# Seven block products in place of eight in the first four K tiles of fourteen block pairs

## The chip, the cores and the metric

The kernel runs on one core of a Trainium2 chip. The metric is the device time of one execution, in microseconds (us). The engines are named as the profile names them: PE (TensorE, matmuls), PEld (its weight loads), DVE (VectorE), ACT (ScalarE), POOL (GpSimd) and SP (the engine whose queue issues most DMAs).

## The reference

Two layers on a sequence of 256 tokens with 2048 features, in float32. Each is followed by a LayerNorm of the residual. The first is a gated MLP with a causal spatial gate, the second is stick-breaking attention with 16 heads.

```python
# layer 1: A_WIDTH 4096, 8 groups of 512 columns, chunks of 128 tokens
h = x @ w_in + b_in                      # w_in: 2048 x 12288
u, v, g = jnp.split(h, 3, axis=-1)
u = jax.nn.gelu(u)
v = layer_norm(jax.nn.gelu(v), vln_g, vln_b)
mixed = jnp.einsum('gts,bcsge->bctge', w, v) + b_s.T[None, None, :, :, None]
y = (u * mixed * jax.nn.silu(g)) @ w_out # 4096 x 2048
x = layer_norm(DN_ALPHA * x + y, ...)
# layer 2
k, v = jnp.split(x @ kv_w, 2, axis=-1)
q, g = jnp.split(x @ w_in, 2, axis=-1)
o = stick_breaking_attention(q, k, v)
x = layer_norm(DN_ALPHA * x + (o * jax.nn.silu(g)) @ w_out, ...)   # w_out: 2048 x 2048
```

## The kernel before

**Products.** A float32 product is made of three matmuls on operands that are split in a high and a low part (`mm3`, L86 to L90: high by high, high by low, low by high). The high part is a cast on ACT (`split`, L77), the low part is a subtraction on DVE (L78). The two token tiles of 128 are the stationary operand, and a matmul streams 512 weight columns. So a block of 512 output columns has two PSUM banks, one for each token tile, and per K tile of 128 rows six matmuls.

**Weights.** `load_chunk` (L115 to L139) loads two K tiles by 512 columns (512 KB) through SP's queue into a tile of the pool `wraw` (4 buffers), and splits it in two tiles of the pool `wspl` (`WB` = 5 buffers of each). `gemm` takes the chunks one after the other.

**Order.** The kernel is written as a program in the Tile framework. A scheduler puts each engine's instructions into an order of its own, by a simulated timeline, and adds the semaphores; the order of an engine's instructions is fixed when the kernel is built. Tiles of one pool and tag take turns in the pool's buffers. Nearly everything of the gated MLP that isn't a weight chunk shares one tag of 26 buffers of 4 KB per partition (pool `big`: the raw x tiles, v, vh and vl, u, g, zh and zl, wsh, wsl and wsr, the residual r, the LayerNorm rows lgb). PSUM has two pools of four banks: `ps_acc` for the products, `ps_aux` for transposes, mixing and attention.

**Stages.** First eight products of 512 columns give v (bias on DVE, Gelu on ACT, statistics on DVE). The spatial weights wsr are loaded and masked, v's LayerNorm factors are worked out. Then for each of 8 groups: v is normalised (L218, L219) and split into vh and vl; two products give u and g; the group's mixing matmuls take vh and vl; u is multiplied by the mix, g by u (`gate`, L305); eight PE transposes of g (L336) and a split give zh and zl, the stationary operand of the output projection. Which of u and g comes first alternates from group to group. After the groups come the output projection of the gated MLP (`residual_gemm`, 4 blocks of 512 columns, 32 K tiles), the first LayerNorm with transposes (xtp, L410), under which the first chunks of the attention's V product run, four rounds of attention (V, K, Q and gate products, and the stick-breaking work of four heads each), the attention's output projection (4 blocks, 16 K tiles) and the last LayerNorm.

Of the kernel before, what the change touches and what calls it, by code (L numbers as in the profile page):

```python
# [9 lines left out]
F32 = mybir.dt.float32  # L10
# [25 lines left out]
ACT_M = (1, 3)  # L36
PINS = {4: (0, 1), 5: (2, 3)}
WARM = 5


@with_exitstack
def trunk_kernel(ctx, tc, x, xT, w_in, b_in, vln_g, vln_b, w_sT, b_sT, w_out, kv_w, bw_in, bw_out, ln_g, ln_b, ln_gT, ln_bT, out):
    nc = tc.nc

    lead = ctx.enter_context(tc.tile_pool(name="lead", bufs=1))
    wraw = ctx.enter_context(tc.tile_pool(name="wraw", bufs=4))
    wspl = ctx.enter_context(tc.tile_pool(name="wspl", bufs=WB))
    big = ctx.enter_context(tc.tile_pool(name="big", bufs=26))
    bcp = ctx.enter_context(tc.tile_pool(name="bcp", bufs=3))
    const = ctx.enter_context(tc.tile_pool(name="const", bufs=1))  # L50
    small = ctx.enter_context(tc.tile_pool(name="small", bufs=4))
    ps_acc = ctx.enter_context(tc.tile_pool(name="ps_acc", bufs=4, space=PSUM))
    ps_aux = ctx.enter_context(tc.tile_pool(name="ps_aux", bufs=4, space=PSUM))

    uid = [0]

# [5 lines left out]
        return big.tile(shape, dt, tag="big", name=nm(s))  # L62

    def aux(s):
        return ps_aux.tile([P, NT], F32, tag="aux", name=nm(s))

    last_w = []

# [65 lines left out]

    def gemm(w, col0, nk, stat, evac, tail=0, head=0, ahead=None, halves=False, cuts=1, after=None):
        w_ = NT // cuts
        accs = [ps_acc.tile([P, w_ if tok else NT], F32, tag="acc", name=nm("acc")) for tok in range(NTOK)]
        wv = w.rearrange("(k p) n -> p k n", p=P)
        nch = nk // CK  # L139
        wh, wl = [None] * nch, [None] * nch  # L140

        def load(c):
            halve = halves and c == 0
            if ahead and not halve:
                ahead(c)
            wh[c], wl[c] = load_chunk(wv, c, col0, spill=nch - tail <= c < nch - WB or c < head - WB, ahead=ahead if halve else None)

        full = [(slice(0, NT), accs[0])], [(slice(0, w_), accs[1])]
        for i in range(1, cuts):
            full[1].append((slice(i * w_, (i + 1) * w_), ps_aux.tile([P, w_], F32, tag="aux", name=nm("acc"))))  # L150
# [24 lines left out]
        for c in range(head):  # L175
            use(c, [1])
        for c in range(head, nch - tail):
            load(c)
            use(c, both)
        for c in range(nch - tail, nch):  # L180
            load(c)
            use(c, [0])
        if tail:
            pins = evac(0, accs[0]) or {}
            for cs, acc in full[1]:
                for c in range(nch - tail, nch):
                    first = use(c, [1], (None, [(cs, acc)]))
                    for t in pins.get(c - (nch - tail), ()):
                        order(t, first)
                evac(1, acc, cs)  # L190
        else:
            for tok in both:
                evac(tok, accs[tok])

    def rsqrt_var(mv, s, fill=None):
        ve = small.tile([P, 1], F32, tag="ve", name=nm("ve"))
# [90 lines left out]
    for n in range(G):  # L287
# [7 lines left out]
            split(vh[:, tok, :], vl[:, tok, :], v[:, tok, :])  # L295

        u = big_tile([P, NTOK, NT], F32, "u")
        ubias = bcast(b_in[n * NT : (n + 1) * NT])

        gt = big_tile([P, NTOK, NT], F32, "g")  # L300
        gbias = bcast(b_in[2 * AW + n * NT : 2 * AW + (n + 1) * NT])
        u_last = n % 2 == 1

        def gate(tok, gt=gt, u=u):
            nc.vector.tensor_tensor(out=gt[:, tok, :], in0=gt[:, tok, :], in1=u[:, tok, :], op=ALU.mult)  # L305

        def evac_u(tok, acc, u=u, bias=ubias, vh=vh, vl=vl, n=n, last=u_last):
            nc.vector.tensor_tensor(out=u[:, tok, :], in0=acc, in1=bias, op=ALU.add)
            nc.scalar.activation(u[:, tok, :], u[:, tok, :], AF.Gelu_apprx_tanh)
            mp = aux("mix")  # L310
            mm3(mp, wsh[:, n, :], wsl[:, n, :], vh[:, tok, :], vl[:, tok, :], True, True)
            nc.vector.scalar_tensor_tensor(out=u[:, tok, :], in0=mp, scalar=bs[:, n : n + 1], in1=u[:, tok, :],
                                           op0=ALU.add, op1=ALU.mult)
            if last:
                gate(tok)

        def evac_g(tok, acc, gt=gt, bias=gbias, last=not u_last):
            nc.vector.tensor_tensor(out=gt[:, tok, :], in0=acc, in1=bias, op=ALU.add)
            nc.scalar.activation(gt[:, tok, :], gt[:, tok, :], AF.Silu)
            if last:  # L320
                gate(tok)

        parts = [(n * NT, evac_u), (2 * AW + n * NT, evac_g)]
        for col0, evac in parts[::-1] if u_last else parts:
            gemm(w_in, col0, KD, xstat, evac)

        zh = big_tile([P, HPT, S], F32R, "zh")
        zl = big_tile([P, HPT, S], F32R, "zl")
# [10 lines left out]
            split(zh[:, hs, :], zl[:, hs, :], tp.rearrange("p (k t) -> p k t", k=2))  # L339


    def residual_gemm(w, nk, stat, rt, layer, finish, fill=None, cuts=1):
        groups = 3 + cuts
        stats = [small.tile([P, groups, 6], F32, tag=f"st{tok}{cuts}", name=nm("st"), bufs=1) for tok in range(NTOK)]
        gb = []

        for n in range(4):
            last = n == 3

            def evac(tok, acc, cs=slice(0, NT), n=n, last=last):  # L350
                r = rt[n][:, tok, cs]
                with tc.high_priority():
                    nc.vector.scalar_tensor_tensor(out=r, in0=r, scalar=ALPHA, in1=acc, op0=ALU.mult, op1=ALU.add)
# [9 lines left out]
            if last:  # L363
                for m in range(4):
                    cs = slice(m * NT, (m + 1) * NT)
                    lt = big_tile([P, 2, NT], F32, "lgb")
                    g, b = lt[:, 0, :], lt[:, 1, :]
                    nc.gpsimd.dma_start(g, ln_g[layer, cs].partition_broadcast(P))
                    nc.gpsimd.dma_start(b, ln_b[layer, cs].partition_broadcast(P))
                    gb.append((g, b))  # L370
            gemm(w, n * NT, nk, stat, evac, tail=TAIL if last else 0, cuts=cuts if last else 1)
        return gb

    xv = x.rearrange("(c p) n -> p c n", p=P)
# [47 lines left out]
    def zstat(k):  # L422
        return zTh[k // HPT][:, k % HPT, :], zTl[k // HPT][:, k % HPT, :]

    gb0 = residual_gemm(w_out, KA, zstat, rt, 0, finish1, fill=fill1)


    nc.vector.memset(tri_f, -1.0)
# [23 lines left out]
                                    compare_op=ALU.is_ge, fill=0.0)  # L452

    sps, wts = [], []
    kw = dict(skip_group_check=True)

    def gemm_T(w, col0, evac, hook=None):
        accs = [ps_acc.tile([P, NT], F32, tag="acc", name=nm("acc")) for _ in range(2)]
# [67 lines left out]
    for j in range(4):  # L526
# [32 lines left out]
        z2s.append((z2h, z2l))  # L559
        for i in range(HPT // 2):  # L560
            weighted(i, v, sg, z2h, z2l)

    def z2stat(k):
        h, l = z2s[k // HPT]
# [18 lines left out]
                steps.append(center(tok, mv, gb, m + 3))  # L583
        order(*steps)

    residual_gemm(bw_out, KD, z2stat, rt, 1, finish2, fill=fill2, cuts=2)
# [38 lines left out]
```

## Time and profile before

| | |
|---|---|
| time, median of 3 runs | 1222.52 us (1222.43 to 1222.58) |
| time of the profiled execution | 1222.06 us |
| its span | 1220.4 us |
| v products | to 182 us |
| u and g products, 8 groups | 182 to 555 us |
| output projection of the gated MLP | 555 to 712 us |
| first LayerNorm | 712 to 750 us |
| attention | 750 to 1121.5 us |
| output projection of the attention | 1121.5 to 1209 us |
| last LayerNorm's end | 1209 to 1220.4 us |

The span runs from the first to the last instruction that the profiler saw; the time of the same execution holds 1.7 us more. Starts are counted from the span's start. Under a name such as `acc<-wh,xTh` stands what is written and what it is made from; in rows of PE the weights (wh, wl) and the tokens (xTh, xTl) are the operands of one matmul. A matmul's shown length (0.39 us) is modelled and overlaps the next one; the distance of starts says how fast matmuls follow each other.

### The profile page before, as it was taken

How to read it: one execution, taken by the hardware profiler on the slowest of the kernel's cores; microseconds unless marked ns; L12 is line 12 of the kernel's file. 1: busy time of each engine (PE TensorE's matmuls, PEld its weight loads, DVE VectorE, ACT ScalarE, POOL GpSimd, SP SyncE). 2: the span in 40 equal slices, each digit the busy share in tenths (PEclk: the TensorE clock that was granted, in tenths of full speed). 3: DMA queues.
4: the chain of work that ended last, by engine and by line, in shares of the span. 5: the costliest groups of instructions: out<-in, count | busy, mean ns of one | idle time of the engine just before them, and what ended most of it. 6: DMA issues, size and time to landing. Idle time of an engine off the chain costs nothing.

```text
span 1220.4 us, 16640 instructions
## 1 busy us (share of the span) xinstructions
PE 1206.5 (99%) x6597; PEld 1053.1 (86%) x6597; DVE 714.7 (59%) x789; ACT 582.7 (48%) x663; POOL 51.5 (4%) x94
## 2 busy tenths in 40 slices
PE   9999999999999999999999999999999999999996
PEld 6888888888888888888888889998998999999885
DVE  6655558667657657655554577455455555546566
ACT  6444445544544544544333455474464455456340
POOL 0000001000000000000000000010010000002000
PEclk9999999999999999999999999999999999999998
DMA  9776777676676677767655655645555655657651
GB/s 307 241 216 202 207 220 238 189 235 205 181 235 206 181 233 222 220 212 247 195 191 195 211 169 174 188 151 173 180 159 167 186 161 156 190 173 203 203 198 69
DMA packets 123694, 240.70 MB, mean 197 GB/s; under 512 B 8129, under 2 KB 11745, under 8 KB 123617
## 3 DMA queue, kind: packets, MB, share of 16 engines
q1 hardware_dynamic: 118848, 224.69, 58.4%
q0 software_dynamic: 4480, 14.70, 4.6%
q8 instruction: 51, 0.84, 0.3%
q10 hardware_dynamic: 288, 0.26, 0.1%
q14 instruction: 27, 0.21, 0.0%
HBM read 237.52 MB, written 2.10 MB: 196 GB/s over the span
## 4 chain that ended last, share of the span: by engine, by line
PE 98%; DVE 1%; DMA 1%; SPq 0%; DVEq 0%; issue 0%
PE acc L89 31%; PE acc L88 31%; PE acc L87 31%; PE ztp L336 1%; DMA xTr<-in_xT 1%; PE zp L501 0%; PE op L88 0%; PE zp L89 0%; PE op L87 0%; PE zp L88 0%; PE op L89 0%; PE zp L87 0%; PE zp L504 0%; PE mix L87 0%; PE mix L89 0%; PE mix L88 0%
## 5 line engine op out<-in xcount | busy, mean ns | idle before, releaser
L78 DVE TENSOR_TENSOR wl<-raw,wh 128x1024 fp32r<-128x1024 f32 (+1 forms) x417 | 507.6, 1223 | 444.0 <-ACT wh L77 442.8
L77 ACT CAST wh<-raw 128x1024 fp32r<-128x1024 f32 (+1 forms) x417 | 437.3, 1051 | 559.3 <-PE acc L89 371.8
L88 PE MATMUL acc<-wl,xTh 128*128 128x512 f32 x896 | 349.7, 391 | 0.0
L87 PE MATMUL acc<-wh,xTh 128*128 128x512 f32 x896 | 348.8, 391 | 0.9 <-ACT xTh L77 0.9
L89 PE MATMUL acc<-wh,xTl 128*128 128x512 f32 x896 | 348.9, 390 | 0.1
L88 PE MATMUL acc<-xTl,wh 128*128 128x256 f32 x768 | 217.4, 283 | 0.0
L87 PE MATMUL acc<-xTh,wh 128*128 128x256 f32 x768 | 217.3, 283 | 0.0
L89 PE MATMUL acc<-xTh,wl 128*128 128x256 f32 x768 | 217.2, 283 | 0.0
L87 PEld LDWEIGHTS acc<-wh,xTh 128*128 128x128 f32 x896 | 168.4, 188 | 36.8 <-ACT xTh L77 2.3
L89 PEld LDWEIGHTS acc<-wh,xTl 128*128 128x128 f32 x896 | 168.5, 188 | 35.2 <-DVE xTl L78 0.5
L88 PEld LDWEIGHTS acc<-wl,xTh 128*128 128x128 f32 x896 | 168.5, 188 | 34.4
L87 PEld LDWEIGHTS acc<-xTh,wh 128*128 128x128 f32 x768 | 147.2, 192 | 0.2
L88 PEld LDWEIGHTS acc<-xTl,wh 128*128 128x128 f32 x768 | 147.2, 192 | 0.2
L89 PEld LDWEIGHTS acc<-xTh,wl 128*128 128x128 f32 x768 | 147.1, 192 | 0.0
L87 PE MATMUL acc<-wh,zh 128*128 128x512 f32 x256 | 99.9, 390 | 0.0
L88 PE MATMUL acc<-wl,zh 128*128 128x512 f32 x256 | 99.7, 390 | 0.0
L89 PE MATMUL acc<-wh,zl 128*128 128x512 f32 x256 | 99.6, 389 | 0.0
L88 PEld LDWEIGHTS acc<-wl,zh 128*128 128x128 f32 x256 | 48.1, 188 | 9.9
L87 PEld LDWEIGHTS acc<-wh,zh 128*128 128x128 f32 x256 | 48.1, 188 | 9.9
L89 PEld LDWEIGHTS acc<-wh,zl 128*128 128x128 f32 x256 | 48.1, 188 | 9.8
L88 PE MATMUL acc<-wl,z2h 128*128 128x512 f32 (+1 forms) x144 | 52.7, 366 | 0.0
L87 PE MATMUL acc<-wh,z2h 128*128 128x512 f32 (+1 forms) x144 | 52.7, 366 | 0.0
(134 smaller groups left out, 745.5 us busy)
## 6 DMA issues: line engine op xcount, KB each, us to landing
raw<-in_w_in SPq DMA_DIRECT2D x191, 512.0 KB, 4.5
raw<-in_w_out SPq DMA_DIRECT2D x64, 512.0 KB, 4.5
raw<-in_kv_w SPq DMA_DIRECT2D x64, 512.0 KB, 3.7
raw<-in_bw_in SPq DMA_DIRECT2D x64, 512.0 KB, 3.8
raw<-in_bw_out SPq DMA_DIRECT2D x32, 512.0 KB, 4.4
bc<-in_b_in POOLq DMA_DIRECT2D x16, 256.0 KB, 4.7
bc<-in_b_in SPq DMA_DIRECT2D x8, 256.0 KB, 4.5
bc<-in_vln_g POOLq DMA_DIRECT2D x8, 256.0 KB, 4.9
```

Source lines behind the costliest of these rows:

```text
L77: h = nc.scalar.copy(hi, src)
L78: return h, nc.vector.tensor_tensor(out=lo, in0=src, in1=hi.bitcast(F32), op=ALU.subtract)
L87: first = nc.tensor.matmul(acc, lhsT=ah, rhs=bh, start=start, stop=False, **kw)
L88: nc.tensor.matmul(acc, lhsT=ah, rhs=bl, start=False, stop=False, **kw)
L89: nc.tensor.matmul(acc, lhsT=al, rhs=bh, start=False, stop=stop, **kw)
L336: nc.tensor.transpose(out=tp[:, (kk * NTOK + tok) * P : (kk * NTOK + tok + 1) * P], in_=gt[:, tok, c : c + P], identity=ident)
```

## The change

In fourteen pairs of 512-column blocks the first four K tiles no longer go through eight products of (token tile, K half, column block) but through seven, by a scheme of the Strassen and Winograd kind. The pairs are: v blocks 2 to 7 (three pairs), u and g of each group (eight), the output projection of the gated MLP (two), and blocks 0 and 1 of the attention's output projection (one). v blocks 0 and 1, blocks 2 and 3 of the last projection and the attention's products stay as they were.

Write a11, a12 for token tile 0 and K tiles 0-1 and 2-3, a21, a22 for token tile 1; x, y for the two column halves of the weights in K tiles 0-1, w, z for those in K tiles 2-3. The products are: P1 = a11·x, Q5 = (a21-a22)·(x+y), P2 = a12·w, P6 = (a21-a22-a11)·(x+y+z), P7 = (a11-a21)·(y+z), Q3 = (a12+a21-a22-a11)·z, Q4 = a22·(x+y+z+w). Each is six matmuls. Four of them (P1, Q5, P6, P7) leave partial sums in a bank that are copied out, by a DVE operation, into the output tile while the bank goes on accumulating (`snap`). The order of the products and of the remaining chunks of the two blocks is that of `plan`.

The sums on the token side are made once for the input, once for z and once for the attention's output (`a_forms`: one DVE addition of 128x1024, four DVE operations of 128x256 and a split). The sums on the weight side are DVE additions in place (128x1024) in the raw tiles. x is loaded into a tile of `big`, y, z and w into tiles of `wraw`. The bias rows of a pair go into a tile of `big`. `wraw` has 5 buffers where it had 4, `big` 25 where it had 26, and the two PSUM pools become one pool of eight banks with one tag. In the groups g is now always the block of half 0, which ends last, and u that of half 1. The LayerNorm rows of the last projections are loaded ahead of the tail.

```diff
+NP = 2
+
+
+def plan(nk, tail=0):
+
+    each = (nk - 2 * NP) // CK
+    one = ["P1", "Q5", "P2", 1, "P6", 1, "P7", 1, 1, "Q3"] + [1] * (each - 4)
+    zero = [0, "Q4"] + [0] * (each - tail - 1)
+    return one + zero
...
-    wraw = ctx.enter_context(tc.tile_pool(name="wraw", bufs=4))
+    wraw = ctx.enter_context(tc.tile_pool(name="wraw", bufs=5))
     wspl = ctx.enter_context(tc.tile_pool(name="wspl", bufs=WB))
-    big = ctx.enter_context(tc.tile_pool(name="big", bufs=26))
+    big = ctx.enter_context(tc.tile_pool(name="big", bufs=25))
...
-    ps_acc = ctx.enter_context(tc.tile_pool(name="ps_acc", bufs=4, space=PSUM))
-    ps_aux = ctx.enter_context(tc.tile_pool(name="ps_aux", bufs=4, space=PSUM))
+    ps = ctx.enter_context(tc.tile_pool(name="ps", bufs=8, space=PSUM))
...
+    def a_forms(h, l, p):
+
+        raw = big_tile([P, 2 * p, S], F32, "ar")
+        nc.vector.tensor_tensor(out=raw, in0=h.bitcast(F32), in1=l.bitcast(F32), op=ALU.add)
+        a11, a21, a12, a22 = [raw[:, k * p : (k + 1) * p, t * P : (t + 1) * P] for k in range(2) for t in range(2)]
+        f = big_tile([P, 4, p, P], F32, "af")
+        fh, fl = big_tile([P, 4, p, P], F32R, "afh"), big_tile([P, 4, p, P], F32R, "afl")
+        for i, (a, b, op) in enumerate([(a21, a22, ALU.subtract), (f[:, 0], a11, ALU.subtract),
+                                        (a11, a21, ALU.subtract), (a12, f[:, 1], ALU.add)]):
+            nc.vector.tensor_tensor(out=f[:, i], in0=a, in1=b, op=op)
+        split(fh, fl, f)
+        return fh, fl
+
+    def block(w, cols, nk, stat, forms, p, plan, snap, final, tail=0, before_tail=None):
+
+
+        wv = w.rearrange("(k p) n -> p k n", p=P)
+        b = [None] * 4
+
+        def load(k, half, keep=False):
+            r = big_tile([P, CK, NT], F32, "sraw") if keep else wraw.tile([P, CK, NT], F32, tag="raw", name=nm("raw"))
+            nc.sync.dma_start(r[:, 0:p, :], wv[:, k : k + p, cols[half] : cols[half] + NT])
+            return r[:, 0:p, :]
...
+        def product(i, src, a):
+            wh = wspl.tile([P, CK, NT], F32R, tag="wh", name=nm("wh"))
+            wl = wspl.tile([P, CK, NT], F32R, tag="wl", name=nm("wl"))
+            split(wh[:, 0:p, :], wl[:, 0:p, :], src)
+            acc, new = bank(i)
+            for j in range(p):
+                ah, al = a(j)
+                mm3(acc, ah, al, wh[:, j, :], wl[:, j, :], new and j == 0, j == p - 1, **kw)
+            return acc
...
+        def P1():
+            raw["x"], raw["y"], raw["z"] = load(0, 0, keep=True), load(0, 1), load(p, 1)
+            snap("P1", product(1, raw["x"], quarter(0, 0)))
+            add(raw["x"], raw["y"])
+
+        def Q5():
+            snap("Q5", product(2, raw["x"], form(0)))
+            add(raw["x"], raw["z"])
+            add(raw["y"], raw["z"])
+
+        def P2():
+            raw["w"] = load(p, 0)
+            product(0, raw["w"], quarter(p, 0))
+
+        def P6():
+            snap("P6", product(1, raw["x"], form(1)))
+            add(raw["x"], raw["w"])
+
+        def P7():
+            snap("P7", product(1, raw["y"], form(2)))
+
+        def Q3():
+            product(2, raw["z"], form(3))
+
+        def Q4():
+            product(1, raw["x"], quarter(p, 1))
...
+        for s in plan:
+            if isinstance(s, str):
+                steps[s]()
+                continue
+            k = left[s].pop(0)
+            wh, wl = load_chunk(wv, k // CK, cols[s])
+            use(s, k, wh, wl, (1, 0) if s else (0, 1))
+            if not left[s]:
+                for tok in range(NTOK):
+                    final(tok, s, b[2 * s + tok])
+        if tail:
+            before_tail()
...
+    def bias_block(w, cols, nk, stat, forms, p, plan, bias, dst, then):
+
+        def snap(name, acc):
+            tok, half = dict(P1=(0, 0), Q5=(1, 1), P6=(0, 1), P7=(1, 1))[name]
+            d = dst(tok, half)
+            if name == "P7":
+                nc.vector.tensor_tensor(out=d, in0=d, in1=acc, op=ALU.subtract)
+            elif name == "P6":
+                nc.vector.tensor_tensor(out=d, in0=bias[half], in1=acc, op=ALU.subtract)
+            else:
+                nc.vector.tensor_tensor(out=d, in0=acc, in1=bias[half], op=ALU.add)
+
+        def final(tok, half, acc):
+            d = dst(tok, half)
+            nc.vector.tensor_tensor(out=d, in0=acc, in1=bias[half] if (tok, half) == (1, 0) else d, op=ALU.add)
+            then(tok, half)
+
+        block(w, cols, nk, stat, forms, p, plan, snap, final)
...
+    def pair_bias(*cols):
+        t = big_tile([P, 2, NT], F32, "pb")
+        for i, c in enumerate(cols):
+            nc.gpsimd.dma_start(t[:, i, :], b_in[c : c + NT].partition_broadcast(P))
+        return [t[:, i, :] for i in range(2)]
...
-    for n in range(G):
+    for n in range(2):
...
+    xforms = a_forms(xTh[:, 0 : 2 * NP, :], xTl[:, 0 : 2 * NP, :], NP)
+    for n in range(2, G, 2):
+        pair = [big_tile([P, NTOK, NT], F32, "v") for _ in range(2)]
+        vt += pair
+        bias = pair_bias(AW + (n + 1) * NT, AW + n * NT)
+
+        def v_then(tok, half, pair=pair, n=n):
+            d = pair[1 - half][:, tok, :]
+            nc.scalar.activation(d, d, AF.Gelu_apprx_tanh)
+            nc.vector.bn_stats(vstats[:, tok, n + 1 - half, :], d)
+
+        bias_block(w_in, (AW + (n + 1) * NT, AW + n * NT), KD, xstat, xforms, NP, plan(KD), bias,
+                   lambda tok, half, pair=pair: pair[1 - half][:, tok, :], v_then)
...
+        cols = (2 * AW + n * NT, n * NT)
+
+        def ug_then(tok, half, gt=gt, u=u, vh=vh, vl=vl, n=n):
+            if half:
+                nc.scalar.activation(u[:, tok, :], u[:, tok, :], AF.Gelu_apprx_tanh)
+                mp = aux("mix")
+                mm3(mp, wsh[:, n, :], wsl[:, n, :], vh[:, tok, :], vl[:, tok, :], True, True)
+                nc.vector.scalar_tensor_tensor(out=u[:, tok, :], in0=mp, scalar=bs[:, n : n + 1], in1=u[:, tok, :],
+                                               op0=ALU.add, op1=ALU.mult)
+            else:
+                nc.scalar.activation(gt[:, tok, :], gt[:, tok, :], AF.Silu)
+                nc.vector.tensor_tensor(out=gt[:, tok, :], in0=gt[:, tok, :], in1=u[:, tok, :], op=ALU.mult)
+
+        bias_block(w_in, cols, KD, xstat, xforms, NP, plan(KD), pair_bias(*cols),
+                   lambda tok, half, gt=gt, u=u: (gt, u)[half][:, tok, :], ug_then)
...
+        def snap(name, acc, n):
+            tok, half = dict(P1=(0, 0), Q5=(1, 1), P6=(0, 1), P7=(1, 1))[name]
+            r = rt[n + 1 - half][:, tok, :]
+            if name == "P7":
+                nc.vector.tensor_tensor(out=r, in0=r, in1=acc, op=ALU.subtract)
+            else:
+                nc.vector.scalar_tensor_tensor(out=r, in0=r, scalar=ALPHA, in1=acc, op0=ALU.mult,
+                                               op1=ALU.subtract if name == "P6" else ALU.add)
...
+            paired = n < 2 or cuts == 1
...
+            if not paired:
+                if last:
+                    load_gb()
+                gemm(w, n * NT, nk, stat, evac, tail=TAIL if last else 0, cuts=cuts if last else 1)
+            elif n % 2:
+                ends = evacs.pop(), evac
+                block(w, (n * NT, (n - 1) * NT), nk, stat, forms, NP, plan(nk, TAIL if last else 0),
+                      lambda name, acc, n=n: snap(name, acc, n - 1),
+                      lambda tok, half, acc, ends=ends: ends[1 - half](tok, acc), tail=TAIL if last else 0, before_tail=load_gb)
+            else:
+                evacs.append(evac)
...
+    zforms = a_forms(zTh[0], zTl[0], NP)
...
+        if j == 0:
+            z2forms = a_forms(z2h, z2l, NP)
```

## Rows read from the trace of the kernel before

**Rows 1.** The page, its first part: each engine's busy time, share of the span, instructions.

```profile
PE 1206.5 (99%) x6597; PEld 1053.1 (86%) x6597; DVE 714.7 (59%) x789; ACT 582.7 (48%) x663; POOL 51.5 (4%) x94
```

**Rows 2.** The page, the chain that ended last: shares of the span by engine.

```profile
PE 98%; DVE 1%; DMA 1%; SPq 0%; DVEq 0%; issue 0%
```

**Rows 3.** Waits: who waited for whom, us in total, times, longest us.

```profile
ACT wh L77 <- PE acc L89: 371.8, 231, 2.0
```

**Rows 4.** Windows, u/g stage: us; busy PE, PEld, DVE, ACT, POOL; clock, DMA, GB/s.

```profile
182.00:555.00 373.00, 373.00 (x1676) 309.09 (x1675) 241.79 (x277) 186.07 (x208) 24.35 (x43) 1.00 0.70 214
```

**Rows 5.** Timeline of PE in the first v product: start, us, instruction.

```profile
14.25 0.39 PE L87 MATMUL acc<-wh,xTh 128*128 128x512 f32 x1
...
14.93 0.39 PE L87 MATMUL acc<-wh,xTh 128*128 128x512 f32 x1
```

**Rows 6.** Instruction groups by form on DVE and ACT: busy, mean ns, idle before.

```profile
L78 DVE TENSOR_TENSOR wl<-raw,wh 128x1024 fp32r<-128x1024 f32 x415 | 506.2, 1225 | 442.6 <-ACT wh L77 441.4
L547 DVE TENSOR_TENSOR r<-r,lgb 128x1024 f32<-128x1024 f32 x4 | 4.9, 1217 | 0.0
L308 DVE TENSOR_TENSOR u<-acc,bc 128x512 f32<-128x512 f32 x16 | 10.3, 682 | 0.0
L78 DVE TENSOR_TENSOR xTl<-xTr,xTh 128x256 fp32r<-128x256 f32 x2 | 0.8, 419 | 0.0
...
L77 ACT CAST wh<-raw 128x1024 fp32r<-128x1024 f32 x415 | 436.0, 1053 | 557.8 <-PE acc L89 371.8 <-PE acc L88 118.7 <-DMA raw<-in_w_in 19.7
```

**Rows 7.** Timeline of SP and DVE around the two spatial tables and v_7's first write.

```profile
12.12 0.34 SPq L273 DMA_DIRECT2D bs<-in_b_sT  x1
...
179.05 0.46 SPq L268 DMA_DIRECT2D wsr<-in_w_sT  x1
...
181.24 1.28 DVE L258 TENSOR_TENSOR v<-acc,bc 128x512 f32<-128x512 f32 x2
```

**Rows 8.** Timeline of DVE, ACT and PE at the boundary of groups 0 and 1.

```profile
204.66 1.41 DVE L219 SCALAR_TENSOR_TENSOR v<-v,vrstd,bc 128x512 f32<-128x512 f32 x2 [1.54 <-DMA bc<-in_vln_b]
...
226.12 1.28 DVE L318 TENSOR_TENSOR g<-acc,bc 128x512 f32<-128x512 f32 x2
227.68 1.28 ACT L319 ACT_TABLE_LOAD   x1
229.64 1.29 DVE L305 TENSOR_TENSOR g<-g,u 128x512 f32<-128x512 f32 x2 [0.72 <-ACT g L319]
234.35 0.82 PE L336 MATMUL ztp<-ident,g 128*128 128x128 f32 x6
234.88 1.08 ACT L77 CAST zh<-ztp 128x512 fp32r<-128x512 f32 x2 [1.73 <-PE ztp L336]
235.84 1.16 ACT L77 CAST vh<-v 128x512 fp32r<-128x512 f32 x2
240.60 1.28 DVE L78 TENSOR_TENSOR zl<-ztp,zh 128x512 fp32r<-128x512 f32 x2
```

**Rows 9.** Timeline of PE, ACT and DVE where the v products end.

```profile
181.98 0.39 PE L89 MATMUL acc<-wh,xTl 128*128 128x512 f32 x1
...
193.72 1.28 ACT L77 CAST vh<-v 128x512 fp32r<-128x512 f32 x2
195.40 1.29 DVE L78 TENSOR_TENSOR vl<-v,vh 128x512 fp32r<-128x512 f32 x2
```

**Rows 10.** Timeline of PE and ACT where the attention ends.

```profile
1121.55 0.40 PE L87 MATMUL acc<-wh,z2h 128*128 128x512 f32 x1
...
1122.53 0.62 ACT L77 CAST z2h<-z 128x512 fp32r<-128x512 f32 x1 [0.22 <-DVE z L522]
```

**Rows 11.** Timeline of PE in the first LayerNorm.

```profile
723.84 0.39 PE L87 MATMUL acc<-wh,xTh 128*128 128x512 f32 x1
...
734.73 1.03 PE L410 MATMUL xtp<-ident,r 128*128 128x128 f32 x8
```

**Rows 12.** Timeline of PE at the start: the five warming matmuls.

```profile
1.99 2.50 PE L111 MATMUL warm<-wz 128*128 128x512 f32 x5 [1.99 <-DVE wz L108]
```

**Rows 13.** Windows behind the last matmul (columns as in rows 4).

```profile
1210.00:1213.00 3.00, 0.00 (x0) 0.00 (x0) 2.93 (x8) 0.20 (x1) 0.00 (x0) 1.00 0.01 2
...
1214.00:1217.00 3.00, 0.00 (x0) 0.00 (x0) 2.92 (x6) 0.00 (x0) 0.00 (x0) 0.50 0.45 173
```

More of the change, by code (lines that the diff above doesn't have):

```diff
@@ L64, in aux @@
     def aux(s):
-        return ps_aux.tile([P, NT], F32, tag="aux", name=nm(s))
+        return ps.tile([P, NT], F32, tag="ps", name=nm(s))
     last_w = []
@@ L136, in gemm @@
         w_ = NT // cuts
-        accs = [ps_acc.tile([P, w_ if tok else NT], F32, tag="acc", name=nm("acc")) for tok in range(NTOK)]
+        accs = [ps.tile([P, w_ if tok else NT], F32, tag="ps", name=nm("acc")) for tok in range(NTOK)]
         wv = w.rearrange("(k p) n -> p k n", p=P)
@@ L149, in gemm @@
         for i in range(1, cuts):
-            full[1].append((slice(i * w_, (i + 1) * w_), ps_aux.tile([P, w_], F32, tag="aux", name=nm("acc"))))
+            full[1].append((slice(i * w_, (i + 1) * w_), ps.tile([P, w_], F32, tag="ps", name=nm("acc"))))
         def use(c, toks, pieces=full):
@@ L193, in gemm @@
                 evac(tok, accs[tok])
+    kw = dict(skip_group_check=True)
+    def a_forms(h, l, p):
[9 more added lines that the diff above has]
+        return fh, fl
@@ new lines, in block, with bank, add, quarter @@
+    def block(w, cols, nk, stat, forms, p, plan, snap, final, tail=0, before_tail=None):
+        wv = w.rearrange("(k p) n -> p k n", p=P)
+        b = [None] * 4
+        def bank(i):
+            if b[i] is None:
+                b[i] = ps.tile([P, NT], F32, tag="ps", name=nm("acc"))
+                return b[i], True
+            return b[i], False
+        def load(k, half, keep=False):
+            r = big_tile([P, CK, NT], F32, "sraw") if keep else wraw.tile([P, CK, NT], F32, tag="raw", name=nm("raw"))
+            nc.sync.dma_start(r[:, 0:p, :], wv[:, k : k + p, cols[half] : cols[half] + NT])
+            return r[:, 0:p, :]
+        def add(dst, src):
+            nc.vector.tensor_tensor(out=dst, in0=dst, in1=src, op=ALU.add)
+        raw = {}
+        def product(i, src, a):
[7 more added lines that the diff above has]
+            return acc
+        def quarter(k0, tok):
+            def a(j):
+                return tuple(t[:, tok * P : (tok + 1) * P] for t in stat(k0 + j))
+            return a
+        def form(i):
+            return lambda j: (forms[0][:, i, j, :], forms[1][:, i, j, :])
+        def P1():
[18 more added lines that the diff above has]
+            product(1, raw["x"], quarter(p, 1))
+        steps = dict(P1=P1, Q5=Q5, P2=P2, P6=P6, P7=P7, Q3=Q3, Q4=Q4)
+        left = {h: [2 * p + c * CK for c in range((nk - 2 * p) // CK)] for h in (0, 1)}
+        def use(half, k0, wh, wl, toks):
+            first = None
+            for j in range(CK):
+                k = k0 + j
+                sh, sl = stat(k)
+                for tok in toks:
+                    ts = slice(tok * P, (tok + 1) * P)
+                    acc, new = bank(2 * half + tok)
+                    m = mm3(acc, sh[:, ts], sl[:, ts], wh[:, j, :], wl[:, j, :], new, k == nk - 1, **kw)
+                    first = first or m
+            return first
+        for s in plan:
[10 more added lines that the diff above has]
+            before_tail()
+            late = []
+            for i, k in enumerate(left[0]):
+                late.append((k, *load_chunk(wv, k // CK, cols[0], spill=i < len(left[0]) - WB)))
+                use(0, *late[-1], (0,))
+            pins = final(0, 0, b[0]) or {}
+            for i, chunk in enumerate(late):
+                first = use(0, *chunk, (1,))
+                for t in pins.get(i, ()):
+                    order(t, first)
+            final(1, 0, b[1])
+        assert len(left[0]) == tail and not left[1]
@@ L297, in trunk_kernel @@
         u = big_tile([P, NTOK, NT], F32, "u")
-        ubias = bcast(b_in[n * NT : (n + 1) * NT])
         gt = big_tile([P, NTOK, NT], F32, "g")
[L301 to L325, printed above, removed]
+        cols = (2 * AW + n * NT, n * NT)
[11 more added lines that the diff above has]
+                   lambda tok, half, gt=gt, u=u: (gt, u)[half][:, tok, :], ug_then)
         zh = big_tile([P, HPT, S], F32R, "zh")
@@ L361, in evac @@
                         return finish(tok, mv, rstd, gb, ins)
[L363 to L371, printed above, removed]
+            if not paired:
[7 more added lines that the diff above has]
+                      lambda tok, half, acc, ends=ends: ends[1 - half](tok, acc), tail=TAIL if last else 0, before_tail=load_gb)
+            else:
+                evacs.append(evac)
         return gb
@@ L423, in zstat @@
         return zTh[k // HPT][:, k % HPT, :], zTl[k // HPT][:, k % HPT, :]
-    gb0 = residual_gemm(w_out, KA, zstat, rt, 0, finish1, fill=fill1)
+    zforms = a_forms(zTh[0], zTl[0], NP)
+    gb0 = residual_gemm(w_out, KA, zstat, zforms, rt, 0, finish1, fill=fill1)
     nc.vector.memset(tri_f, -1.0)
@@ L454, in trunk_kernel @@
     sps, wts = [], []
-    kw = dict(skip_group_check=True)
     def gemm_T(w, col0, evac, hook=None):
-        accs = [ps_acc.tile([P, NT], F32, tag="acc", name=nm("acc")) for _ in range(2)]
+        accs = [ps.tile([P, NT], F32, tag="ps", name=nm("acc")) for _ in range(2)]
         wv = w.rearrange("(k p) n -> p k n", p=P)
@@ L584, in finish2 @@
         order(*steps)
-    residual_gemm(bw_out, KD, z2stat, rt, 1, finish2, fill=fill2, cuts=2)
+    residual_gemm(bw_out, KD, z2stat, z2forms, rt, 1, finish2, fill=fill2, cuts=2)
 _INS = ["x", "xT", "w_in", "b_in", "vln_g", "vln_b", "w_sT", "b_sT", "w_out", "kv_w", "bw_in", "bw_out", "ln_g", "ln_b", "ln_gT", "ln_bT"]
```

18 lines of the change are left out of this document (14 added, 4 removed).

## The prediction

> **What bounds the kernel now.** I read the page first. PE is busy 99% of the span, the next engine is DVE with 59% [rows 1], and the chain that ended last lies on PE for 98% [rows 2]. The waits say the same from the other side: the casts of the weight chunks wait for a matmul to give a buffer back, 231 times for 371.8 us [rows 3], so the feeders are ahead of PE. The windows show it for the stage with most of the pairs: PE 373.00 of 373.00 us, DVE 241.79, ACT 186.07, clock 1.00 [rows 4]. So time falls if matmuls go away, and rises by every microsecond in which PE finds nothing to do. At present it always finds something: behind the last matmul of a product the next chunks lie split in five pairs of buffers. The question is whether that holds where a pair begins.
>
> **What is removed.** Matmuls start 0.68 us apart over three intervals, 0.227 us each [rows 5]. Eight products of six become seven: 6 fewer per pair, 84 in 14 pairs, 84 x 0.227 = 19.0 us. The profiled execution took 1222.06 us (the median of the runs is 1222.52, 0.04% more), so without any new wait 1203.
>
> **What is added off PE.** A pair gets three more splits (19 for 16, 1.225 us each on DVE), four additions of 128x1024 (1.217, from the nearest row of that form) and four copies of partial sums (0.682) [rows 6]: 3.7 + 4.9 + 2.7 = 11.3 us of DVE per pair. In the group stage that makes 241.79 + 8 x 11.3 = 332 us of about 362, 92%. By these durations it still fits, so I cost it at nothing; the cover is PE's 45 us per pair, and it goes if the additions come late (rival 3). ACT's three casts more (1.053 each) fit easily. SP issues as many weight bytes as before.
>
> **In what order tiles are handed out.** This is the step on which my forecast rests. wsr and bs are two loads in a row of the program on one queue. bs has a place of its own and is issued at 12.12 us; wsr, a tile of `big`, is issued at 179.05, when the first write of v_7 (181.24), the tile of `big` ahead of it in the program, is near [rows 7]. The queue was open and the pool was far from full at 12 us. The same is seen at the boundaries of groups: the v of group 1 was normalised at 204.66, but its vh is cast at 235.84, right behind zh of group 0 at 234.88, with ACT idle for 1.73 us just before [rows 8]; it is so at all seven. I read this as a rule of the scheduler: the tiles of one tag get their buffers in the order in which the program first writes them, even when buffers are free. Now x of a pair is a tile of `big`, behind zh and zl of the group before and vh and vl of its own. And P1's split is the first of its pair to take buffers of `wspl`, so Q5, P2 and the plain chunks can't be split before it; with one PSUM tag its bank also comes after the transposes' banks. So at the start of a pair PE has nothing that lies ready: it waits for the evacuation of g, the gating, the transposes, and the splits up to x. ACT runs these casts in the order given.
>
> [...]
>
> **The seven starts between groups.** Evacuation, Silu and multiplication: from 226.12 to 229.64 + 1.29 = 230.93, less the table load of 1.28 that can run beside the evacuation: 3.5 us. First four transposes about 0.5 (six took 0.82). zh 1.08, vh 1.16 for both halves [rows 8]. Cast of x 1.05, its subtraction 1.22 [rows 6]. Together 8.5, less 0.9 of transposes that PE does anyway: 7.6. P1 then covers 6 x 0.227 = 1.36 us, but Q5 needs x + y (1.22), a cast and a subtraction, 3.5 in all: 2.1 idle. P2's split ends about 2.3 behind Q5's cast, Q5 covers 1.36: 1.0 more. Sum 10.7, seven times 74.9.
>
> **The other four starts.** From v to the groups: the last v matmul starts at 181.98, the vh casts end at 195.0 [rows 9]; of the 12.8 us some four weight casts (4.2) would go away, 8.6; with x's split 10.9, with the 3.1 of Q5 and P2 14.0. From v block 1 to the first pair: evacuation 1.28, token sums 1.22 + 4 x 0.42, their cast 1.05, x's split 2.27: 7.5, and 3.1: 10.6 [rows 6]. From the groups to the projection: 5.1 to zh, 1.3 to zl [rows 8], token sums and cast 3.95, x's split 2.27, less 0.9, plus 3.1: 14.7. From attention to its projection: matmuls now start at 1121.55 on split chunks, the last cast of z2h ends at 1123.15 [rows 10]; x's split behind it makes 3.9, plus 3.1: 7.0. Pairs 2 and 3 of v and pair 2 of the projection have nothing but bank copies ahead of them; I cost them at nothing, covered by the plain chunks of the pair before.
>
> **One PSUM tag.** In the first LayerNorm the head chunks of V run from 723.84 on, ahead of the last transposes at 734.73 [rows 11]. With one tag in program order their banks come behind those transposes: between 8 and 11 us, I take 10. In the attention's four rounds the gate product's banks come behind the scores': about two copies of a bank (0.68 each), 4 x 1.4 = 5.6; nothing at the low end.
>
> **Sum.** -19.0 + 74.9 + 14.0 + 10.6 + 14.7 + 7.0 + 10 + 5.6 = +117.8; 1222.06 + 117.9 = 1340.
>
> Bounds of a start: if P1's matmuls go ahead on the cast alone and Q5 and P2 find their splits made, 3.1 less each, 34 less; with the PSUM terms at nothing 50 less: 1290. Upwards: the table load not hidden, 7 x 1.28 = 9; and the clock. [...] The likeliest case's own range is 1285 to 1385. [...]
>
> [...]
>
> **The rivals.**
>
> 1. *Faster: the order doesn't bind at the starts.* If x is loaded and split while the group before still runs, PE goes on. For it speaks that ACT and DVE have room ahead of each boundary; against it the late wsr and vh. Then only the 19.0 come off, less about 3 for the first token sums: 1222.1 - 19.0 + 3 = 1206. It decides from 19.0/11 = 1.7 us per start: below that the kernel gets faster, above it slower.
> 2. *The starts stop, but P2 and a plain chunk fill them.* If buffers of `wspl` go to whoever is ready, P2 (1.36 us) and one chunk (2.7) run while x is waited for, and with PSUM free in the same way its terms go. The starts' 121.2 less 11 x 4.1 is 76: 1222.1 - 19.0 + 76 = 1279. Against it: I have no row in which a later chunk overtook an earlier one.
> 3. *The starts are clean, but DVE eats the gain.* With 92% by durations, additions between products (add, cast, subtract: 3.5 us against products of 1.36) can come late. 1.36 us per pair gives the 19.0 back: 1222, no change.
>
> **How the numbers follow.** Chances: forecast 0.45, rival 2 0.22, rival 1 0.26, rival 3 0.07. A change of 0.2% (2.4 us) is about what a measurement of this kernel can tell from none. Forecast and rival 2 are slower: 0.67, and 0.01 of rival 3: 0.68. Rival 1 and a part of rival 3 are faster: 0.28. The same: 0.04. The range starts below rival 1, at 1203, holds rivals 2 and 3, and ends at 1370, where a quarter of the forecast's cases and some of rival 1's are left out.
>
> **What would show it.** Right: PE idle for 7 to 12 us at each of seven boundaries, waiting for the cast or the subtraction of P1's wh and wl, with these behind vh on ACT; 6,597 - 84 = 6,513 matmuls; DVE over 85% in the group stage; a gap of 8 to 11 us ahead of the second half's transposes. Wrong: a load of x issued, and cast, well before zh of the group before. Then the reading of the order is at fault, and the time falls to rival 1. If PE waits inside the pairs instead, for the additions, it is rival 3.

## The result and the profile after

The changed kernel takes 1343.05 us (median of 4 runs, 1341.01 to 1344.82) against 1222.47: ratio 1.0986, 95% interval 1.0967 to 1.1005. The forecast was 1340.

The page of the kernel after, engines and chain (as in [rows 1, 2]):

```profile
PE 1235.7 (92%) x6513; PEld 1052.0 (79%) x6513; DVE 872.4 (65%) x961; ACT 631.1 (47%) x715; POOL 57.7 (4%) x100
...
PE 80%; DVE 10%; issue 5%; DMA 2%; ACT 2%; SPq 0%; POOL 0%; DVEq 0%; ACTq 0%; POOLq 0%
```

84 matmuls are gone, yet PE is busy 29 us longer, and a fifth of the chain lies elsewhere. The timeline of the kernel after at the boundary of groups 0 and 1, from SP, PE, DVE and ACT, answers to [rows 8]:

```profile
251.64 0.47 SPq L234 DMA_DIRECT2D sraw<-in_w_in  x1
...
261.37 0.39 PE L98 MATMUL acc<-wh,xTl 128*128 128x512 f32 x1
262.50 1.37 DVE L480 TENSOR_TENSOR g<-g,u 128x512 f32<-128x512 f32 x2
263.34 0.41 PE L494 MATMUL ztp<-ident,g 128*128 128x128 f32 x2 [1.58 <-DVE g L480]
264.51 1.07 ACT L86 CAST zh<-ztp 128x512 fp32r<-128x512 f32 x2 [1.36 <-PE ztp L494]
265.48 1.15 ACT L86 CAST vh<-v 128x512 fp32r<-128x512 f32 x2
266.51 1.05 ACT L86 CAST wh<-sraw 128x1024 fp32r<-128x1024 f32 x1
267.60 1.23 DVE L87 TENSOR_TENSOR wl<-sraw,wh 128x1024 fp32r<-128x1024 f32 x1
267.62 0.80 PE L96 MATMUL acc<-wh,xTh 128*128 128x512 f32 x1 [2.81 <-ACT wh L86]
268.86 1.23 DVE L238 TENSOR_TENSOR sraw<-sraw,raw 128x1024 f32<-128x1024 f32 x1
268.88 0.80 PE L97 MATMUL acc<-wl,xTh 128*128 128x512 f32 x1 [0.46 <-DVE wl L87]
...
269.90 0.63 PE L96 MATMUL acc<-wh,xTh 128*128 128x512 f32 x1
270.18 1.05 ACT L86 CAST wh<-sraw 128x1024 fp32r<-128x1024 f32 x1 [2.61 <-DVE sraw L238]
270.33 0.63 PE L97 MATMUL acc<-wl,xTh 128*128 128x512 f32 x1
271.26 1.22 DVE L87 TENSOR_TENSOR wl<-sraw,wh 128x1024 fp32r<-128x1024 f32 x1
271.27 0.80 PE L96 MATMUL acc<-wh,afh 128*128 128x512 f32 x1
```

The load of x (`sraw`) is issued at 251.64, 15 us before its cast. The cast comes behind zh and vh, as forecast, and PE stops three times, 4.85 us together. Behind the third stop matmuls start 0.43 us apart, not 0.227; the last row is Q5's first matmul. The windows of the same stretch (columns as in [rows 4]) say why: the granted clock.

```profile
261.00:262.00 1.00, 0.76 (x4) 0.29 (x2) 0.88 (x2) 0.16 (x1) 0.00 (x0) 1.00 0.00 0
...
266.00:267.00 1.00, 0.00 (x0) 0.00 (x0) 1.00 (x3) 1.00 (x3) 0.00 (x0) 0.87 0.79 184
...
270.00:271.00 1.00, 1.00 (x4) 0.56 (x2) 0.96 (x2) 0.82 (x1) 0.00 (x0) 0.50 0.00 0
...
274.00:275.00 1.00, 1.00 (x6) 0.80 (x5) 1.00 (x2) 0.00 (x0) 0.00 (x0) 1.00 0.00 0
```

It falls to 0.50 at 266.7, some 5 us behind the last full row of matmuls (the last one started at 261.37), and is back at 1.00 at 273.6. So half of a start's price of 9.5 us is not in the stops that the trace shows; what the slow matmuls have in it is asked in experiment 3. The forecast, term by term (each measured one is the stretch between the same two events in both traces, plus what its fewer matmuls save):

| term | forecast | measured | from, to |
|---|---|---|---|
| first pair of v | 10.6 | 12.0 | last v matmul 181.98, 189.94 |
| start of the groups | 14.0 | 28.4 | first add of g_0 226.12, 261.12 |
| seven starts between groups | 74.9 | 66.8 | last group's add 545.39, 637.66 |
| start of the projection | 14.7 | 12.3 | its last matmul 723.61, 825.50 |
| first LayerNorm | 10 | 9.4 | first K matmul 745.14, 856.43 |
| attention's gate products | 5.6 | 1.4 | last gate matmul 1118.55, 1231.27 |
| its projection | 7.0 | 7.3 | last matmul's end 1209.44, 1328.05 |
| end | 0 | 0.3 | span 1220.4, 1339.3 |
| sum, less 19.0 of matmuls | 117.8 | 118.9 | |

In the kernel before the projection's matmuls run until 724 us, and not until 712 as the table of stages has it; the term goes by its last matmul.

The start of the groups is twice its forecast. Timeline of PE and DVE there, after:

```profile
199.89 0.80 PE L96 MATMUL acc<-wh,xTh 128*128 128x512 f32 x1 [9.57 <-ACT wh L86]
200.73 1.40 DVE L368 SCALAR_TENSOR_TENSOR v<-v,vmv,bc 128x512 f32<-128x512 f32 x2
202.06 0.68 DVE L87 TENSOR_TENSOR vl<-v,vh 128x512 fp32r<-128x512 f32 x1
202.66 1.41 DVE L369 SCALAR_TENSOR_TENSOR v<-v,vrstd,bc 128x512 f32<-128x512 f32 x2
203.98 1.21 DVE L87 TENSOR_TENSOR wl<-sraw,wh 128x1024 fp32r<-128x1024 f32 x1
205.25 0.79 PE L97 MATMUL acc<-wl,xTh 128*128 128x512 f32 x1 [4.56 <-DVE wl L87]
```

P1 has its wh at 199.9 and waits 4.56 us for wl, because DVE first finishes group 0's vl and normalises v of later groups (L368, L369). In each window of 4 us from 200 to 228 DVE is busy 4.00. Before, the same work was spread under running matmuls.

### The profile page after: what moved, and what is told of

It reads as the page before. It is cut to its first block, busy times and chain, and to the rows that moved or that the text cites. A ratio compares the mean times of both kernels' runs of the same rounds, so it can differ in the third digit from the quotient of the medians.

```text
span 1339.3 us, 16717 instructions
## 1 busy us (share of the span) xinstructions
PE 1235.7 (92%) x6513; PEld 1052.0 (79%) x6513; DVE 872.4 (65%) x961; ACT 631.1 (47%) x715; POOL 57.7 (4%) x100
## 4 chain that ended last, share of the span: by engine, by line
PE 80%; DVE 10%; issue 5%; DMA 2%; ACT 2%; SPq 0%; POOL 0%; DVEq 0%; ACTq 0%; POOLq 0%
PE acc L96 26%; PE acc L97 25%; PE acc L98 25%; DVE wl L87 2%; DMA raw<-in_w_in 2%; DVE sraw L238 2%; ACT wh L86 1%; DVE g L480 1%; DVE g L340 1%; DVE zl L87 1%; DVE vl L87 1%; DVE raw L238 0%; DVE v L368 0%; PE zp L683 0%; DVE v L369 0%
## 5 line engine op out<-in xcount | busy, mean ns | idle before, releaser
L87 DVE TENSOR_TENSOR wl<-raw,wh 128x1024 fp32r<-128x1024 f32 (+1 forms) x403 | 487.8, 1222 | 267.6 <-ACT wh L86 264.4
L86 ACT CAST wh<-raw 128x1024 fp32r<-128x1024 f32 (+1 forms) x403 | 415.9, 1048 | 392.1 <-PE acc L98 178.3
L96 PE MATMUL acc<-wh,xTh 128*128 128x512 f32 x786 | 310.0, 404 | 41.6 <-ACT wh L86 38.6
L97 PE MATMUL acc<-wl,xTh 128*128 128x512 f32 x786 | 313.0, 398 | 10.2 <-DVE wl L87 10.1
L98 PE MATMUL acc<-wh,xTl 128*128 128x512 f32 x786 | 310.6, 396 | 0.0
L97 PEld LDWEIGHTS acc<-wl,xTh 128*128 128x128 f32 x786 | 150.3, 191 | 47.4 <-DVE wl L87 16.5
L98 PEld LDWEIGHTS acc<-wh,xTl 128*128 128x128 f32 x786 | 150.7, 192 | 30.9
L86 ACT CAST wh<-sraw 128x1024 fp32r<-128x1024 f32 x56 | 58.9, 1051 | 98.3 <-DVE sraw L238 66.2
L98 PE MATMUL acc<-wh,zl 128*128 128x512 f32 x236 | 92.3, 391 | 0.0
L87 DVE TENSOR_TENSOR wl<-sraw,wh 128x1024 fp32r<-128x1024 f32 x56 | 68.4, 1221 | 14.5 <-ACT wh L86 14.5
L96 PEld LDWEIGHTS acc<-wh,zh 128*128 128x128 f32 x236 | 44.5, 189 | 16.2 <-ACT wh L86 7.2
L96 PE MATMUL acc<-wh,afh 128*128 128x512 f32 x112 | 49.4, 441 | 4.2 <-ACT wh L86 4.2
```

Source lines behind the costliest of these rows:

```text
L86: h = nc.scalar.copy(hi, src)
L87: return h, nc.vector.tensor_tensor(out=lo, in0=src, in1=hi.bitcast(F32), op=ALU.subtract)
L96: first = nc.tensor.matmul(acc, lhsT=ah, rhs=bh, start=start, stop=False, **kw)
L97: nc.tensor.matmul(acc, lhsT=ah, rhs=bl, start=False, stop=False, **kw)
L98: nc.tensor.matmul(acc, lhsT=al, rhs=bh, start=False, stop=stop, **kw)
```

## The experiments

Experiments 2, 3, 5, 6 and 9 have one run each; the runs of a kernel that has more lie up to 5 us apart.

**1. x in a pool of its own.**

```diff
-    big = ... bufs=25
+    big = ... bufs=24
+    xraw = ctx.enter_context(tc.tile_pool(name="xraw", bufs=1))
-            r = big_tile([P, CK, NT], F32, "sraw") if keep else ...
+            r = xraw.tile([P, CK, NT], F32, tag="sraw", ...) if keep else ...
```

> x of each pair lies in a pool of its own with one buffer (the large pool has 24 then), nothing else differs from the changed kernel. Order theory (the tiles of one tag are handed out in program order, so x and all behind it wait for zh and vh of the group boundary): P1, Q5, P2 and two chunks are cast ahead of zh, a start between groups stops only for the gating ahead of the transposes, about 1.6 us, and the clock stays up, so 9.3 us per start become 2 to 3; with the other four starts about 85 us less than 1343, 1250 to 1270. DVE theory (the added additions, copies and splits hold PE up): x's place changes nothing, 1330 or more.

1303.19 us, ratio 1.0659 (1.0643 to 1.0675): 40 us back, not 73 to 93. Timeline of ACT and PE at a boundary of this kernel, and windows:

```profile
337.57 1.05 ACT L87 CAST wh<-sraw 128x1024 fp32r<-128x1024 f32 x1 [1.71 <-issue]
...
347.70 0.39 PE L99 MATMUL acc<-wh,xTl 128*128 128x512 f32 x1
352.03 0.66 PE L495 MATMUL ztp<-ident,g 128*128 128x128 f32 x2 [3.94 <-DVE g L481]
352.34 0.78 PE L97 MATMUL acc<-wh,xTh 128*128 128x512 f32 x1
```

```profile
351.00:352.00 1.00, 0.00 (x0) 0.00 (x0) 0.81 (x2) 0.68 (x2) 0.00 (x0) 0.50 0.01 2
...
354.00:355.00 1.00, 1.00 (x3) 0.76 (x3) 0.00 (x0) 0.00 (x0) 0.00 (x0) 0.50 0.18 31
```

P1's weights now lie split long before (x is cast at 337.57), but its first matmul comes directly behind the first write of the transposes' banks, 3.94 us late, and the clock is down. That is the other tag: with one PSUM pool P1's bank comes behind theirs. I had put this order into the reading but not into the expectation's price.

**2. Two PSUM pools again.** `ps` with four banks for the products, `ps_aux` with four for `aux` and the cut last block; x stays in `big`.

> The changed kernel with two PSUM pools of four banks again (products; transposes, mixing, attention). Order theory: the head chunks of V fill the first LayerNorm again, the gap of 7.7 us there and its slow matmuls go, 9 us less than 1343, 1334; the starts of pairs stay as they are, since x is still behind zh and vh. Rival (the gap is DVE work of the LayerNorm): no change, 1343.

1325.76 us, 17 less where 9 were expected. V's head chunks lie under the first LayerNorm again (its last projection matmul to the first of K: 21.5 us as before). The starts gain 0.8 each as well, since the mixing matmuls now fill part of the stop. Alone it is a small part: x still holds the starts.

**3. Matmuls without use in the stop.** Behind the last split of zh, for seven groups:

```diff
+        if n < G - 1:
+            dummy = aux("dummy")
+            for i in range(14):
+                nc.tensor.matmul(dummy, lhsT=zh[:, 0, 0:P], rhs=xTh[:, 0:2, :]..., ...)
```

> The changed kernel with 14 matmuls without use (512 columns, 0.227 us each at full clock, 3.2 us) behind the first cast of zh at each of the seven boundaries between groups, where PE now stops for 2.8 us. Clock theory (about half of a start's 9.3 us is the half clock behind the stop): the clock stays at its full level, each start costs 3 to 4 us less, 21 to 28 less in all, 1315 to 1322. Rival (the clock costs little, the stop and the waits for splits are all): the added matmuls do nothing or cost 0.4 us each time, 1343 to 1346.

1347.8 us, 5 more: a miss for the clock theory. Timeline and windows of PE:

```profile
318.72 0.41 PE L494 MATMUL ztp<-ident,g 128*128 128x128 f32 x2 [1.58 <-DVE g L480]
...
320.53 3.47 PE L501 MATMUL dummy<-xTh,zh 128*128 128x512 f32 x14 [0.35 <-ACT zh L86]
323.84 0.39 PE L96 MATMUL acc<-wh,xTh 128*128 128x512 f32 x1
...
326.66 0.49 PE L96 MATMUL acc<-wh,afh 128*128 128x512 f32 x1 [0.96 <-ACT wh L86]
327.61 0.51 PE L96 MATMUL acc<-wh,xTh 128*128 128x512 f32 x1 [0.45 <-ACT wh L86]
328.55 0.79 PE L96 MATMUL acc<-wh,xTh 128*128 128x512 f32 x1 [0.44 <-ACT wh L86]
```

```profile
324.00:325.00 1.00, 0.96 (x5) 0.65 (x4) 0.97 (x2) 0.00 (x0) 0.00 (x0) 1.00 0.63 139
...
329.00:330.00 1.00, 1.00 (x4) 0.71 (x4) 1.00 (x2) 0.00 (x0) 0.00 (x0) 0.50 0.00 0
```

The clock stands at 1.00 in the window behind the dummies, and at 0.50 in the one from 329 to 330, behind the short waits for the splits of Q5, P2 and the chunk (0.96, 0.45 and 0.44 us); why it falls there is not shown. The fall, in the window from 328 to 329 (0.73), comes about 9.7 us behind the first transpose, in place of 1.3 at this boundary of the changed kernel (317.93 for 316.67), so this kernel doesn't give the price of a whole start. It does price the slow P1. Q5's first matmul starts 7.93 us behind the first transpose at each of the seven starts of the changed kernel, with P1 at half clock. Here it starts 7.94 us behind it (326.66 for 318.72), with the clock at 1.00 in the window after P1's first matmul. So P1's slow matmuls cost nothing: they lie under the addition, cast and subtraction for Q5. Behind Q5's first matmul, one to eight matmuls of a start of the changed kernel are still at half clock, and the 45th instruction of PE behind the first transpose comes at 16.1 us with one of them and at 17.1 with eight. So the clock has at most about 1 us in a start's 9.5, and the rival of the expectation is nearer.

**4. Both: x in its own pool and two PSUM pools.**

> Both edits: x in its own pool and two PSUM pools. Order theory: P1's bank no longer waits for the transposes' banks either, so the starts between groups cost nearly nothing, and the first LayerNorm is filled again: 15 to 25 us below the kernel with x alone in its pool, 1230 to 1245; what is left is the start of the groups (about 15 us), where DVE normalises v. DVE theory: 1320 or more.

1258.63 us, ratio 1.0305 (1.0288 to 1.0322): 14 over the expected bounds, and far from the DVE theory's 1320. No stop of more than 0.4 us is left at six of the seven boundaries, and the spacing of the groups' transposes falls from 53.8 to 46.3 us (45.8 before). So the two orders together are 7.5 of the 9.5 us of a start between groups. Left are a stop of 7.8 us at the first pair and 6.3 at the projection, both for the token sums, and the start of the groups.

**5. The kernel before with one PSUM pool, no product changed.**

> The kernel before, with nothing changed but its two PSUM pools of four banks put together into one pool of eight banks with one tag. Order theory: at the end of each of the eight groups the next product's bank comes behind the transposes' banks, so PE stops about 4 us for the gating and then runs about 3 us slower at half clock, 8 x 6.8 = 54; the first LayerNorm loses 9 and the attention 1: 1280 to 1295, with no product changed at all. The prediction's own term (10 in the LayerNorm and 5.6 in the attention, nothing at the groups) would give 1238.

1277.22 us, 55 more, a little under the expected bounds (its starts cost 5.5 each, not 6.8, and the first LayerNorm 10). Of the 5.5, 3.9 are the stop; in the other 1.6 seven to nine instructions of PE run at half clock. Timeline of PE at its first boundary:

```profile
225.88 0.39 PE L88 MATMUL acc<-wh,xTl 128*128 128x512 f32 x1
230.16 0.52 PE L335 MATMUL ztp<-ident,g 128*128 128x128 f32 x2 [3.89 <-DVE g L304]
230.33 0.78 PE L86 MATMUL acc<-wh,xTh 128*128 128x512 f32 x1
```

Here the order of a tag is shown by itself: all else is that of the kernel before, which ran through its groups without a stop [rows 4].

**6. Token sums earlier.** On top of experiment 4, `a_forms` of the input stands behind v block 0, that of z ahead of zh of group 7.

> x in its own pool, two PSUM pools, and the token sums made earlier in the program: those of the input behind v block 0, those of z ahead of the last group's transposes. Theory (stop plus half clock, both gone when the sums lie ready): the first pair's start loses nothing instead of 7.8 us of stop and some 5 of slow matmuls, the projection's start 6.3 of stop and some 5; 1258.6 becomes 1232 to 1238. Rival (the stops move on to the next split): 1250 or more.

1238.36 us, the upper end of what was expected; both stops are gone.

**7. Normalisation held back.** On top of 6, `order` puts the normalisation of group n behind the last product's split of the pair ahead, and the mixing matmuls behind u's last chunk.

> As before with the early token sums, and also v of groups 1 to 7 is normalised only behind the last product of the pair ahead on DVE, and the mixing matmuls come behind the last chunk of u on PE. Theory (at the start of the groups DVE is full with the normalisations of later groups, and PE stands behind the mixing matmuls): 10 to 15 us less than with the early sums alone, 1218 to 1226, about the time of the kernel before. Rival (the wait is the chain of statistics and the first normalisation): 3 us less at most.

1244.44 us, ratio 1.0169 (1.0149 to 1.0189): worse, a miss. At each boundary P6 now waits 1.57 us (9.1 at the first) for the copy of P1 into g: g is a tile of `big` behind vh and vl, which came late. That is the same rule, one tile further on; experiment 8 moves vh and vl, and the wait is gone.

**8. The normalisation written later in the program.** On top of 6: vh, vl and the next pair's bias rows stand behind P7, so that g and u come ahead of them in `big`.

> x in its own pool, two PSUM pools, early token sums, and the normalisation and split of a group's v written in the program behind product P7 of the pair (where the mixing needs them soon), with the bias rows of the next pair behind them; nothing on DVE is held back. Order theory: the copies of P1 and Q5 into g and u no longer come behind vh and vl, so the start of the groups costs 2 to 4 us instead of 14 and each group loses its small waits around vl (1 to 1.5 us): 1212 to 1222, at or below the kernel before. Rival (DVE is too full in the groups): 1230 or more.

1226.83 us, ratio 1.0042 (1.0028 to 1.0056): 12 less than 6, but not below before, and between the theory's bounds and the rival's. The crowd on DVE moved to the first boundary (stops of 0.4 to 2.0 us from 226 to 245).

**9. The same without the additions.**

> The same without the four additions of the weight side per pair, so that the products are made of x, y and z instead of their sums (part of the computation is left out; matmuls, splits and copies stay): 4.9 us of DVE less per pair. DVE theory (the additions on DVE hold PE up): 10 us or more below the kernel with them. Order theory: within 3 us of it.

1218.12 us, 8.7 less: near the DVE theory's 10, not the other's 3. The groups' spacing falls from 45.4 to 44.9 us, so the additions hold PE up by about 0.5 us in a group. More than half of the 8.7 comes at one place, the crowded first boundary (50.7 to 46.0 us between the first two groups' transposes). An addition is DVE time and also a step between two products; this run doesn't tell the two apart.

**10. Normalisation of one group at a time,** held behind P7 of the pair ahead.

> The kernel with the late normalisation, and on DVE the normalisation of group n's v is also held behind the split of product P7 of the pair ahead. Theory (what is left at the start of the groups, about 8 us of stops and 4 of slow matmuls, is DVE full with normalisations of later groups): 8 to 12 us less, 1214 to 1219, below the kernel before. Rival (it is the first group's own chain of statistics, normalisation, gate): 1224 or more.

1224.21 us, ratio 1.0015 (1.0006 to 1.0024). The start of the groups is mended (the first transposes at 230.4 us, 236.5 in experiment 8, 233.9 in the kernel before), but five boundaries have a new stop of 1.3 us for a wl behind the normalisation.

**11. The same behind Q3 of the own pair.**

```diff
+                if hook and s == "Q3":
+                    hook()        # normalise, vh, vl, bias rows of the next pair
...
+                    order(marks["split"], norm)
```

> The kernel with late and held normalisation, but a group's v is normalised behind the split of product Q3 of its own pair (written there in the program and held there on DVE), in place of behind P7 of the pair ahead, which came to lie at the start of the pair. Theory (the stop of 1.3 us at each start between groups is the weight split behind the normalisation on DVE, so it goes when the normalisation lies in the middle of the pair): the groups' spacing falls from 46.5 to 44.5 to 45 us, the start of the groups stays as it is, 1212 to 1216, 0.5 to 0.8% below the kernel before. Rival (DVE is too full anywhere in the pair): 1221 or more.

1217.91 us, ratio 0.9964 (0.9952 to 0.9977): below both kernels. Page, window of the group stage, and the one stop per group that is left:

```profile
PE 1193.8 (98%) x6513; PEld 1036.0 (85%) x6513; DVE 869.6 (71%) x961; ACT 633.9 (52%) x715; POOL 56.2 (5%) x100
```

```profile
182.00:555.00 373.00, 366.12 (x1628) 298.58 (x1626) 328.15 (x374) 217.57 (x240) 19.41 (x35) 1.00 0.64 209
```

```profile
278.37 0.51 PE L99 MATMUL acc<-wl,xTh 128*128 128x512 f32 x1 [0.61 <-DVE wl L89]
```

The time is a little over the expectation. The spacing is 45.9 us, that of before, and not 44.5 to 45: in the groups nothing is left of the 1.36 us per pair. Of it 0.6 shows as the stop for a wl from DVE, which is busy 88% there; the rest is in waits that a matmul's shown length covers, and what they wait for is not shown.

## Why the prediction was right, and where it was not

**The order of the tags: right, and shown.** Taking x out of `big` and P1's bank out of the transposes' pool removes 84 us of the 121 lost; either alone removes 40 and 17. One PSUM pool alone costs the old kernel 55. That the same rule binds g behind vh was seen in experiments 7 and 8. One thing in it came otherwise. The step lets x, as a tile of `big`, come behind zh, but its load was issued at 251.64, 13 us before zh was cast; only the cast came in the forecast place. So the order holds PE up through the sequence of casts on ACT, and why it leaves the load free is not shown.

**What a start is made of: about right, a little over-sized.** The step "Sum 10.7" came to 9.5. From the first add of g to P1's wl it laid out 8.5 us, and 7.7 were measured (261.12 to 268.83): casts and transposes on ACT, DVE and PE overlap (zh's first cast starts at 264.51, the transposes end at 264.81; zl's subtraction starts at 265.13, zh's second cast ends at 265.59), while I laid them end to end. From there to Q5's wl it laid out 3.5, and 3.65 were measured (to 272.48); but Q5 began on its cast alone, at 271.27. The sign "PE idle for 7 to 12 us" did not come in that form: the trace shows 4.85 us of idle, in part because the slow matmuls of P1 fill the wait for Q5.

The clock has no term in the sum. The top of the likeliest case's range has one: 1340, 9 for the table load and 36 for the clock, 3.3 at each of eleven starts, are 1385. That was my estimate, and no run shows it. Behind ten of the eleven starts the granted clock did stand at 0.50, for 6.8 to 20.5 us, but at a start between groups this cost at most about 1 us (experiment 3): of the 73 instructions of PE that start at half clock at the seven starts, 42 come ahead of Q5's first matmul, under the wait for its split. Over the whole kernel PE's idle time grew from 2.9 to 92.3 us (summed over the timeline). With 19.0 saved, 48.5 of the 118.9 are not shown as idle: slow matmuls, by my estimate 23 us at most (126 instructions of PE start at half clock, 0.2 us more for 512 columns), and waits that a matmul's shown length covers.

**Luck.** The right total owes something to errors that met: the start of the groups came 14.4 us over its term, the starts between groups 8.1 under, the gate products 4.2 and the projection's start 2.4 under. Two sums are off by 0.1 (14.7 for 14.8, 117.9 for 117.8), which changes nothing.

**The start of the groups: mis-sized by half.** 28.4 for 14.0. "Some four weight casts would go away" looked at ACT alone; the work that came in their place was on DVE, the normalisation of later groups, and the sum had no term for it. Experiments 10 and 11 show it: with this work held apart, the first transposes come at 230.4 and 228.8 us, and the start's loss is gone.

**The gate products' banks: 1.4 for 5.6.** The low end, nothing, was nearer. The first LayerNorm came to 9.4 for 10, and its gap ahead of the second half's transposes is 7.7 us, just under the 8 to 11 foreseen. **Token sums** (the two starts that wait for them): 12.0 and 12.3 for 10.6 and 14.7, and gone when made earlier.

**DVE at nothing: right for the result, wrong as a rule.** Between the groups of the changed kernel little shows of it, since the starts hide it; DVE was 286.32 of 415 us busy from 223 to 638, not over 85%. With the starts mended, what remains looks like rival 3: experiment 9 gets 8.7 us by leaving out the additions, and the last kernel keeps 4.6 of the 19 us.

## What to carry to other kernels

In a framework that gives buffers of a tag in program order, ask of each new tile what stands ahead of it under the same tag, data apart, and give its own pool to whatever a later stage needs first (40 us in experiment 1; one PSUM pool cost the kernel before 55 in experiment 5). Price the slow matmuls behind a stop only where PE would otherwise run on: in experiment 5 they came with 1.6 us on top of a stop of 3.9, in the changed kernel most of those at the seven starts lay under the next wait. And what ran unseen under a busy engine has to be counted where it lands when that engine stops: here DVE's normalisations, at the start of the groups (28.4 us for 14.0).

## What the runs showed of the hardware

The granted clock fell without one unbroken stop, too. In the kernel after it fell at 266.7 though PE had run eight transposes from 263.3 to 264.8. In experiment 3 it stood at 1.00 from 324 to 325 and at 0.50 from 329 to 330, behind a run of waits of 0.96, 0.45 and 0.44 us with one matmul between each. In experiment 1 it stood at 0.50 from 351 to 352, within a single stop of 3.94 us that ended at 352.03. In the first of these falls the clock stood at 0.50 for 6.8 us, most of them with matmuls running, before it was 1.00 again.
